# Scaling softmax exponentials on GpSimd in a two-layer encoder: a per-partition scalar operand in place of a broadcast tensor operand

## The chip, the cores and the metric

One core of one Trainium2 chip. The metric is the device time of one execution in microseconds (us), the median of several runs. Engines are named as in the profile: PE (TensorE matmul), PEld (its weight loads), DVE (VectorE), ACT (ScalarE), POOL (GpSimd), SP (SyncE, which issues nearly all DMAs).

## The reference, cut to what matters

Two layers run over 512 tokens of width 1024, in float32. Each layer projects x, mixes tokens with 16 attention heads of three kinds (6 latent heads, 6 dilated ones with a bias, 4 grouped-query ones), projects the result, normalises, and runs a SwiGLU feed-forward part. What the change touches is the softmax of each head; the grouped and latent heads compute it as

```
logits = jnp.einsum('bqkgd,bskd->bkgqs', qblk, k).astype(jnp.float32) * scale
p = jax.nn.softmax(logits, axis=-1)
return jnp.einsum('bkgqs,bskd->bqkgd', p.astype(v.dtype), v)
...
x = layer_norm(DN_ALPHA * x + mix, ln1_g[l], ln1_b[l])
ff = (jax.nn.silu(x @ ffn_w_gate[l]) * (x @ ffn_w_up[l])) @ ffn_w_down[l]
```

The dilated heads compute a mixture of three masked softmaxes, which the kernel folds into one softmax with a bias table per head.

## The kernel before, in words

A float32 product is made of three matmuls on a high and a low part of each operand (`mm3`, L159 to L167). `wload` (L142) loads a weight tile, lets ACT round it to the high part (`whi`, L152), and lets DVE or POOL subtract to get the low part (`wlo`, L156).

Attention works in units: one head and one block of 128 queries, so 64 units in a layer. `Head` has three steps for a unit. Step `a` (L236) makes the scores `sc` on PE (L241), the row minimum of the negated scores on DVE (`nm`, L247 with a bias table, L251 without one), the exponentials `pl` with their row sum on ACT (L253), the reciprocal `srec` on DVE (L255), and scales `pl` in place on POOL (L256). Step `b` (L259) transposes the scaled tile on PE (`ptr`, L264) and splits it into `PTh` (ACT, L271) and `PTl` (DVE, L272). Step `c` (L274) multiplies by the values (`po`, L282 and L283), and L288 and L290 put the halves together.

`attend` (L312) calls step `a` of unit u, step `b` of unit u-3 and step `c` of unit u-4, and between them pieces of other work, the fillers: projections of the later heads (`tp`, `qkp`, `uq`, `uv`), transposes (`tT`, `lt`), and part of the output projection (`opp`). The fillers have a due range of units in the table `W`. `evac_g1` (L460) scales and rotates a projected block `g1` on DVE (L470, L471, L474 to L477), after POOL made its `rstd` (L191, L192). `layer_norm` (L195) and `finish` close the attention part. Then comes the feed-forward part, which uses no step of `Head`.

The order of the program text isn't the order of execution. The kernel is built with `schedule_with_timeline_sim=True`: a scheduler orders the instructions of each engine by the text's priority and by what it believes each takes. On the chip each engine then works through its own list strictly in that order and waits where an operand isn't ready.

Buffers that matter here: 4 tiles for `pl` (pool `ppl`, shared with some scratch tiles), 2 PSUM banks for scores (`ps_sc`), 2 for the transposes (`ps_pt`), and one tile `gg` for the per-head gains (pool `pgg`), which is loaded again for the second layer in the middle of the first one's attention (L406) and scaled there on DVE (L407).

Of the kernel before, what the change touches and what calls it, by code (L numbers as in the profile page):

```python
# [13 lines left out]
ALU = mybir.AluOpType  # L14
AX = mybir.AxisListType

P = 128
T = 512
# [63 lines left out]
def encoder(ctx: ExitStack, tc, x, w_in, mla_q_norm, mla_kv_norm, w_uq, w_ukv, gqa_q_norm, gqa_k_norm, rel_bias,  # L82
            w_out, ln1_g, ln1_b, w_gate, w_up, w_down, ln2_g, ln2_b, tabs, onehot, neglnc, out):
    nc = tc.nc
    V, A, G, TE = nc.vector, nc.scalar, nc.gpsimd, nc.tensor
# [27 lines left out]
    def bank(pl, name):  # L113
        return pl.tile([P, 512], F32, tag="b", name=name)

    def small(n, name):
        return psm.tile([P, n], F32, tag="s", name=name)
# [44 lines left out]
    def mm3(ps, a, b, first, last):  # L162
        ah, al = a
        bh, bl = b
        TE.matmul(ps, ah, bh, start=first, stop=False)  # L165
        TE.matmul(ps, ah, bl, start=False, stop=False)  # L166
        TE.matmul(ps, al, bh, start=False, stop=last)  # L167
# [63 lines left out]
    class Head:  # L231
# [4 lines left out]
        def a(self, qt):  # L236

            sc = bank(ps_sc, "sc")
            ops = self.qk(qt)
            for i, (a, b) in enumerate(ops):  # L240
                TE.matmul(sc, a, b, start=i == 0, stop=i == len(ops) - 1)  # L241
            pl = ppl.tile([P, T], F32, tag="l", name="pl")
            nm = small(1, "nm")
            src = sc
            if self.dtile is not None:
                o = 895 - (384 - P * qt)
                V.tensor_tensor_reduce(out=pl, in0=sc, in1=self.dtile()[:, slice(o, o - T if o >= T else None, -1)], scale=1.0, scalar=3e38,  # L247
                                       op0=ALU.add, op1=ALU.min, accum_out=nm)
                src = pl
            else:  # L250
                V.tensor_reduce(nm, sc, axis=AX.X, op=ALU.min)  # L251
            s = small(1, "ssum")
            A.activation(pl, src, AF.Exp, bias=nm, scale=-1.0, accum_out=s)  # L253
            r = small(1, "srec")
            V.reciprocal(r, s)  # L255
            G.tensor_tensor(pl, pl, r.to_broadcast([P, T]), op=ALU.mult)  # L256
            self.pl[qt] = pl

        def b(self, qt):  # L259
# [133 lines left out]
    for l in range(DEPTH):  # L393
# [143 lines left out]
        def dil_qk(pair):  # L537
            ws = [wload(krows(w_in[l], 0, KD, c + pair * P, c + pair * P + P), (P, KD, P), LO['qk'], QKR[pair]) for c in (C_Q, C_K)]
            yield
            for q, (h, o) in zip((True, False), ws):  # L540
                pb = bank(ps_mm, "qkp")
                for k in range(KD):
                    mm3(pb, (h[:, k], o[:, k]), xmv(xT, k), k == 0, k == KD - 1)
                    if k % 2 and k < KD - 1:
                        yield

                if q:
                    r = pqk.tile([P, 2, T], F32R, tag="q", name="dqk")
                    sc = -(HD ** -0.5)
                    for e in range(2):  # L550
                        a, b = slice(64 * e, 64 * e + 64), slice(64 - 64 * e, 128 - 64 * e)
                        A.activation(r[a, e], pb[a], AF.Copy, scale=sc)
                        V.scalar_tensor_tensor(r[b, e], pb[a], sc, r[a, e].bitcast(F32), op0=ALU.mult, op1=ALU.subtract)
                    dqk[pair].append(r)
                else:
                    for e in range(2):
                        r = (pmix if e else pqk).tile([P, 2, T], F32R, tag="m" if e else "q", name="dk")
                        a, b = slice(64 * e, 64 * e + 64), slice(64 - 64 * e, 128 - 64 * e)
                        A.copy(r[a, 0], pb[a])
                        V.tensor_tensor(r[a, 1], pb[a], r[a, 0].bitcast(F32), op=ALU.subtract)  # L560
                        nc.sync.dma_start(r[b].bitcast(F32), r[a].bitcast(F32))
                        dqk[pair].append(r)
                yield
# [10 lines left out]
        def latent_qv():  # L574
            q = pxt.tile([P, NT, 6, 96], F32, tag="x", name="tq")
            tq.append(q)
            wq = [wload(krows(w_uq[l], 0, 2, 288 * c, 288 * c + 288), (P, 2, 288), LO['uq']) for c in range(2)]
            wkv.append(wload(krows(w_ukv[l], 0, 1, 0, 768), (P, 1, 768), LO['kv']))
            yield
            for c in range(2):  # L580
                h, o = wq[c]
                for t in range(NT):
                    pb = bank(ps_mm, "uq")[:, :288]
                    ts = slice(t * P, (t + 1) * P)
                    for k in range(2):
                        mm3(pb, (latT[k][:, 0, ts], latT[k][:, 1, ts]), (h[:, k], o[:, k]), k == 0, k == 1)
                    A.copy(q[:, t, 3 * c:3 * c + 3, :], pb.rearrange("p (h c) -> p h c", h=3))
                    yield
                tm = ppl.tile([P, T], F32, tag="l", name="qrt")[:, :384].rearrange("p (t h c) -> p t h c", t=NT, h=3)
                rope32(q[:, :, 3 * c:3 * c + 3, 64:96], 3, tm)  # L590
                told.append(("q", c))
            h, o = (w[:, 0].rearrange("p (h c) -> p h c", h=6)[:, :, HD:] for w in wkv[0])
            for t in range(NT):
                pb = bank(ps_mm, "uv")[:, :6 * HD]
                ts = slice(t * P, (t + 1) * P)
                mm3(pb, (latT[2][:, 0, ts], latT[2][:, 1, ts]), (h, o), True, True)
                vt = pv_sb.tile([P, 6, 2, HD], F32R, tag="v", name="mv")
                split_v(vt, pb.rearrange("p (a c) -> p a c", a=6))
                mv_.append(vt)
                yield  # L600

        def out_part():

            def load(half):
                wk = {}
                for k0, n in ((3, 2), (5, 1), (6, 2)):
                    w = wload(krows(w_out[l], k0, n, half * 512, half * 512 + 512), (P, n, 512), LO['opp'])
                    for j in range(n):
                        wk[k0 + j] = (w[0][:, j], w[1][:, j])
                return wk  # L610

            wk = load(0)
            yield
            for half in range(2):
                cs = slice(half * 512, half * 512 + 512)
                for t in range(NT):
                    ts = slice(t * P, (t + 1) * P)
                    pb = bank(ps_mm, "opp")
                    for i, k in enumerate((3, 4, 5, 6, 7)):
                        mm3(pb, (mix[k][:, 0, ts], mix[k][:, 1, ts]), wk[k], i == 0, i == 4)  # L620
                        if i in (1, 3):
                            yield
                    V.scalar_tensor_tensor(xt[:, t, cs], xt[:, t, cs], ALPHA, pb, op0=ALU.mult, op1=ALU.add)
                    told.append(("op", t, half))
                    if half == 0 and t == NT - 1:
                        wk = load(1)
                    yield
# [65 lines left out]
        lqv, op = latent_qv(), out_part()  # L693
# [73 lines left out]
        for part, nf in enumerate((12, 10)):  # L767
# [51 lines left out]
            for half in range(2):  # L819
# [4 lines left out]
                for toks in ((0, 1), (2, 3)) if last else ((0, 1, 2, 3),):  # L824
                    acc = [bank(ps_mm if t < 2 else ps_pv, "down") for t in toks]
                    down(acc, toks, half, LO["dl"] if last else V, LEAD if last else 0)
                    for t, pb in zip(toks, acc):
                        V.scalar_tensor_tensor(xt[:, t, cs], xt[:, t, cs], 1.0 if part else ALPHA, pb,
                                               op0=ALU.mult, op1=ALU.add)
# [35 lines left out]
```

## Time and profile before

| | us |
|---|---|
| median of 3 runs | 1281.85 (1281.53 to 1283.26) |
| the profiled execution, its own time | 1282.31 |
| span of the profiled execution | 1280.5 |
| PE busy in the span | 1250.1 |
| DVE busy | 687.7 |
| ACT busy | 543.6 |
| POOL busy | 324.6 |
| L256 on POOL, 128 instructions | 135.7 |

The span is the time from the first to the last instruction that the trace shows; the execution's own time is 1.8 us longer. Times in the trace count from the start of the span. The first layer's attention units run from about 58 to 265, the second's from about 660 to 892; the feed-forward parts lie between and behind them. Busy times of engines overlap. PE's busy time is a union of pipelined matmuls, so an interval between two matmuls says more than the duration of one.

### The profile page before, as it was taken

What the parts mean: (1) busy time and instruction counts of PE and PEld (TensorE: products, weight loads), DVE (VectorE), ACT (ScalarE), POOL (GpSimd) and SP (SyncE); (2) the same over time, 40 slices, a digit from 0 to 9 for tenths busy, and PEclk for the clock granted to TensorE, in tenths of its full rate; (3) what the DMA queues carried; (4) which work ended last, traced back from release to release, by engine and by line L of the source; (5) the groups of instructions that cost most, each with busy time, mean ns of one, the idle gap of its engine ahead of it and who ended that gap; (6) DMA issues with size and microseconds to landing.
All of it is one profiled execution on the core that took longest, in us unless ns stands there. A gap on an engine that the chain in (4) does not pass through costs nothing.

```text
span 1280.5 us, 16743 instructions
## 1 busy us (share of the span) xinstructions
PE 1250.1 (98%) x6352; PEld 1062.5 (83%) x6352; DVE 687.7 (54%) x1138; ACT 543.6 (42%) x955; POOL 324.6 (25%) x344
## 2 busy tenths in 40 slices
PE   8999899999999999999999998999999999999997
PEld 7888788889888888888898897888988888888885
DVE  4377997684333333332664889966843332333346
ACT  4465786544222212222245668855342221222222
POOL 0445475661000000000245456655500000000004
PEclk9999899999999999999999999999999999999999
DMA  5623210324333233332425231114243333333223
GB/s 179 188 67 87 87 34 13 120 69 130 99 99 97 89 96 98 99 99 99 148 78 147 84 103 48 28 30 134 77 115 99 99 99 99 99 99 98 92 96 110
DMA packets 140552, 122.57 MB, mean 96 GB/s; under 512 B 6924, under 2 KB 114572, under 8 KB 140472
## 3 DMA queue, kind: packets, MB, share of 16 engines
q1 hardware_dynamic: 140460, 121.48, 32.0%
q8 instruction: 50, 0.82, 0.3%
q14 instruction: 30, 0.25, 0.1%
q10 hardware_dynamic: 12, 0.02, 0.0%
HBM read 114.65 MB, written 2.12 MB: 91 GB/s over the span
## 4 chain that ended last, share of the span: by engine, by line
PE 80%; DVE 8%; DMA 4%; ACT 3%; POOL 2%; issue 2%; SPq 0%; DVEq 0%; POOLq 0%; ACTq 0%
PE gate L165 6%; PE down L167 6%; PE down L166 6%; PE up L167 6%; PE down L165 6%; PE up L165 6%; PE up L166 6%; PE gate L167 6%; PE gate L166 6%; PE sc L241 4%; PE ptr L264 3%; PE po L283 2%; PE po L282 2%; PE tp L166 1%; PE tp L165 1%
## 5 line engine op out<-in xcount | busy, mean ns | idle before, releaser
L152 ACT CAST whi<-wraw 128x1024 fp32r<-128x1024 f32 (+3 forms) x202 | 205.6, 1020 | 550.6 <-PE gate L166 149.3
L156 DVE TENSOR_TENSOR wlo<-wraw,whi 128x1024 fp32r<-128x1024 f32 (+3 forms) x170 | 208.2, 1226 | 319.7 <-ACT whi L152 315.7
L191 POOL TENSOR_TENSOR rstd<-mv,eps_l 128x1 f32<-128x1 f32 x16 | 5.7, 357 | 680.8 <-DVE mv L200 680.8
L256 POOL TENSOR_TENSOR pl<-pl,srec 128x512 f32<-128x512 f32 x128 | 135.7, 1061 | 153.0 <-DVE srec L255 139.2
L166 PE MATMUL gate<-xTl,whi 128*128 128x512 f32 (+1 forms) x384 | 142.8, 372 | 0.0
L166 PE MATMUL up<-xTl,whi 128*128 128x512 f32 (+1 forms) x384 | 142.7, 372 | 0.0
L167 PE MATMUL gate<-xTh,wlo 128*128 128x512 f32 (+1 forms) x384 | 142.7, 372 | 0.0
L167 PE MATMUL up<-xTh,wlo 128*128 128x512 f32 (+1 forms) x384 | 142.7, 372 | 0.0
L165 PE MATMUL up<-xTh,whi 128*128 128x512 f32 (+1 forms) x384 | 142.6, 372 | 0.0
L165 PE MATMUL gate<-xTh,whi 128*128 128x512 f32 (+1 forms) x384 | 142.4, 371 | 0.0
L167 PE MATMUL down<-whi,act 128*128 128x512 f32 x352 | 136.7, 389 | 0.0
L166 PE MATMUL down<-wlo,act 128*128 128x512 f32 x352 | 136.7, 389 | 0.0
L165 PE MATMUL down<-whi,act 128*128 128x512 f32 x352 | 136.7, 389 | 0.0
L779 DVE TENSOR_TENSOR sg<-sg,up 128x512 f32<-128x512 f32 x44 | 30.3, 688 | 136.1 <-PE up L167 134.8
L156 POOL TENSOR_TENSOR wlo<-wraw,whi 128x512 fp32r<-128x512 f32 (+2 forms) x64 | 79.4, 1265 | 78.7 <-ACT whi L152 78.4
L272 DVE TENSOR_TENSOR PTl<-ptr,PTh 128x512 fp32r<-128x512 f32 x128 | 87.2, 682 | 8.7 <-ACT PTh L271 7.6
L271 ACT CAST PTh<-ptr 128x512 fp32r<-128x512 f32 x128 | 74.9, 586 | 38.9 <-PE ptr L264 38.4
L167 PEld LDWEIGHTS up<-xTh,wlo 128*128 128x128 f32 x384 | 72.4, 189 | 12.6
L165 PEld LDWEIGHTS gate<-xTh,whi 128*128 128x128 f32 x384 | 72.3, 188 | 12.5
L166 PEld LDWEIGHTS up<-xTl,whi 128*128 128x128 f32 x384 | 72.3, 188 | 12.5
L166 PEld LDWEIGHTS gate<-xTl,whi 128*128 128x128 f32 x384 | 72.4, 188 | 12.4
L165 PEld LDWEIGHTS up<-xTh,whi 128*128 128x128 f32 x384 | 72.3, 188 | 12.4
(174 smaller groups left out, 2493.6 us busy)
## 6 DMA issues: line engine op xcount, KB each, us to landing
wraw<-in_ffn_w_down SPq DMA_DIRECT2D x54, 512.0 KB, 3.6
wraw<-in_ffn_w_up SPq DMA_DIRECT2D x44, 512.0 KB, 3.9
wraw<-in_ffn_w_gate SPq DMA_DIRECT2D x44, 512.0 KB, 3.9
wraw<-in_w_in SPq DMA_DIRECT2D x20, 512.0 KB, 4.7
wraw<-in_w_out SPq DMA_DIRECT2D x14, 512.0 KB, 3.7
dt<-tdr SPq DMA_DIRECT2D x12, 448.0 KB, 3.9
wraw<-in_w_in SPq DMA_DIRECT2D x8, 416.0 KB, 3.4
wraw<-in_w_in SPq DMA_DIRECT2D x8, 384.0 KB, 3.9
```

What stands on the lines that cost most here:

```text
L152: A.copy(h[:, :n], r[:, :n])
L156: lo.tensor_tensor(o[:, c:c + step], r[:, c:c + step], h[:, c:c + step].bitcast(F32), op=ALU.subtract)
L165: TE.matmul(ps, ah, bh, start=first, stop=False)
L166: TE.matmul(ps, ah, bl, start=False, stop=False)
L167: TE.matmul(ps, al, bh, start=False, stop=last)
L241: TE.matmul(sc, a, b, start=i == 0, stop=i == len(ops) - 1)
L256: G.tensor_tensor(pl, pl, r.to_broadcast([P, T]), op=ALU.mult)
L264: TE.transpose(pb[:, kt * P:(kt + 1) * P], pl[:, kt * P:(kt + 1) * P], ident)
L271: A.copy(ph[:, :, c:c + P], pb)
L272: V.tensor_tensor(plo[:, :, c:c + P], pb, ph[:, :, c:c + P].bitcast(F32), op=ALU.subtract)
L282: TE.matmul(po[:, h0:h0 + 256], self.vst(kt), ph[:, kt], start=kt == 0, stop=False)
L779: V.tensor_tensor(sg, sg, pss[1], op=ALU.mult)
```

## The change

The scaling of `pl` becomes a `tensor_scalar` with the column `r` as a scalar per partition; before it was a `tensor_tensor` whose second operand was `r`, repeated along the row. The result is the same product, in place.

```
             r = small(1, "srec")
             V.reciprocal(r, s)
-            G.tensor_tensor(pl, pl, r.to_broadcast([P, T]), op=ALU.mult)
+            G.tensor_scalar(pl, pl, r, None, op0=ALU.mult)
             self.pl[qt] = pl
```

No other line differs. But the scheduler orders the program anew, and the lists of all engines differ in many places. Three of them follow. The number behind a name tells one tile from another of that name.

PE in the first layer, where the grouped-query heads pass over to the latent ones (`sc_2118` is the last grouped unit's scores, `sc_2158` and `sc_2177` are the first two latent ones, `pl_2007` an earlier unit's exponentials). Before:

```order
L264 MATMUL ptr_2129<-tab_114,pl_2007 128x128 x4
L283 MATMUL po_2062<-PTl_2059,gv_801 128x256
L282 MATMUL po_2062<-PTh_2058,gv_852 128x256
L283 MATMUL po_2062<-PTl_2059,gv_852 128x256
L282 MATMUL po_2062<-PTh_2058,gv_1089 128x256
L283 MATMUL po_2062<-PTl_2059,gv_1089 128x256
L282 MATMUL po_2062<-PTh_2058,gv_1125 128x256
L283 MATMUL po_2062<-PTl_2059,gv_1125 128x256
L241 MATMUL sc_2158<-kT_2035,qkT_2001 128x512
L264 MATMUL ptr_2170<-tab_114,pl_2045 128x128 x4
```

Now:

```order
L283 MATMUL po_2062<-PTl_2059,gv_1125 128x256
L241 MATMUL sc_2177<-kT_2035,qkT_2001 128x512 x3
L264 MATMUL ptr_2129<-tab_114,pl_2007 128x128 x4
L504 MATMUL tT_2207<-tab_114,tq_1607 96x128 x4
L165 MATMUL kT_2234<-lat_1785,whi_1622 64x512
L166 MATMUL kT_2234<-lat_1785,whi_1622 64x512
L167 MATMUL kT_2234<-lat_1785,wlo_1624 64x512
L264 MATMUL ptr_2170<-tab_114,pl_2045 128x128 x4
L264 MATMUL ptr_2189<-tab_114,pl_2088 128x128 x4
L241 MATMUL sc_2215<-kT_2035,qkT_2001 128x512 x3
```

The transposes of `pl_2007` stood ahead of the scores `sc_2158`; now they stand behind `sc_2158` (which is further up) and `sc_2177`.

DVE in the first layer, around the last blocks of `g1` (`g1_1423` is the tile of blocks 2 and 3, `PTl_1456` the low part of a unit's transposed exponentials). Before:

```order
L247 ISA pl_1442,nm_1443<-sc_1439,dt_1314 128x512
L247 ISA nm_1443 128x1
L470 TENSOR_SCALAR g1_1423<-g1_1423,rstd_1429 128x256
L471 TENSOR_SCALAR g1_1423<-g1_1423,rstd_1429 128x128
L255 RECIPROCAL srec_1447<-ssum_1445 128x1
L474 TENSOR_TENSOR krt_1484<-g1_1423,tab_114 128x16
L475 TENSOR_TENSOR krt_1484<-g1_1423,tab_114 128x16
L476 TENSOR_TENSOR g1_1423<-g1_1423,tab_114 128x32
L272 TENSOR_TENSOR PTl_1456<-ptr_1500,PTh_1455 128x4x128
```

Now:

```order
L247 ISA pl_1442,nm_1443<-sc_1439,dt_1314 128x512
L247 ISA nm_1443 128x1
L272 TENSOR_TENSOR PTl_1456<-ptr_1500,PTh_1455 128x4x128
L507 TENSOR_TENSOR qkT_1544<-tT_1539,qkT_1544 128x512
L255 RECIPROCAL srec_1447<-ssum_1445 128x1
L474 TENSOR_TENSOR krt_1484<-g1_1423,tab_114 128x16
L475 TENSOR_TENSOR krt_1484<-g1_1423,tab_114 128x16
L476 TENSOR_TENSOR g1_1423<-g1_1423,tab_114 128x32
```

`PTl_1456` moved up ahead of L474 to L476; L470 and L471 moved behind, out of this piece.

POOL at the same place (`wlo_2466` is a low part of an output-projection weight). Before:

```order
L256 TENSOR_TENSOR pl_1350<-pl_1350,srec_1355 128x512
L309 TENSOR_TENSOR mix_1378<-mf_1189,mix_1378 128x512
L256 TENSOR_TENSOR pl_1396<-pl_1396,srec_1401 128x512
L191 TENSOR_TENSOR rstd_1429<-ms_1426,eps_r_118 128x2
L192 TENSOR_TENSOR rstd_1429<-rstd_1429,mhalf_117 128x2
L156 TENSOR_TENSOR wlo_2466<-wraw_2462,whi_2464 128x512 x2
L256 TENSOR_TENSOR pl_1442<-pl_1442,srec_1447 128x512
```

Now:

```order
L256 TENSOR_SCALAR pl_1350<-pl_1350,srec_1355 128x512
L156 TENSOR_TENSOR wlo_2466<-wraw_2462,whi_2464 128x512 x2
L256 TENSOR_SCALAR pl_1396<-pl_1396,srec_1401 128x512
L309 TENSOR_TENSOR mix_1378<-mf_1189,mix_1378 128x512
L191 TENSOR_TENSOR rstd_1429<-ms_1426,eps_r_118 128x2
L256 TENSOR_SCALAR pl_1442<-pl_1442,srec_1447 128x512
```

The pair of `wlo_2466` moved up by one scaling; the operation itself has changed its kind from TENSOR_TENSOR to TENSOR_SCALAR.

## Rows read from the trace of the kernel before

**Rows 1.** The page: span, and busy time of each engine with its share.
```profile
span 1280.5 us, 16743 instructions
...
PE 1250.1 (98%) x6352; PEld 1062.5 (83%) x6352; DVE 687.7 (54%) x1138; ACT 543.6 (42%) x955; POOL 324.6 (25%) x344
```

**Rows 2.** Busy us of each engine by stretch, with instructions and the granted clock.
```profile
core 0: us, PE busy (x) PEld busy (x) DVE busy (x) ACT busy (x) POOL busy (x), PEclk, DMA share, GB/s
...
300.00:600.00 300.00, 300.00 (x1356) 249.81 (x1355) 103.09 (x109) 84.42 (x102) 0.00 (x0) 1.00 0.33 99
...
58.00:265.00 207.00, 198.75 (x1159) 172.63 (x1157) 161.02 (x339) 139.46 (x312) 117.30 (x126) 0.98 0.27 77
660.00:892.00 232.00, 226.77 (x1297) 197.15 (x1297) 173.13 (x355) 155.94 (x332) 121.21 (x130) 0.99 0.29 81
...
160.00:185.00 25.00, 24.19 (x172) 22.07 (x171) 22.78 (x43) 22.76 (x54) 20.20 (x21) 1.00 0.13 43
...
230.00:265.00 35.00, 34.91 (x189) 29.06 (x187) 21.71 (x42) 21.24 (x41) 24.47 (x21) 1.00 0.50 151
```

**Rows 3.** The same view for line L256 alone: us of the stretch, POOL's busy us.
```profile
58.00:265.00 207.00, 68.25 (x64) 0.98 0.27 77
...
160.00:185.00 25.00, 11.46 (x11) 1.00 0.13 43
...
230.00:265.00 35.00, 9.37 (x8) 1.00 0.50 151
```

**Rows 4.** POOL's groups by shape (L156: 230 to 265 only): busy us, mean ns, idle.
```profile
L256 POOL TENSOR_TENSOR pl<-pl,srec 128x512 f32<-128x512 f32 x128 | 135.7, 1061 | 153.0 <-DVE srec L255 139.2 <-PE ptr L264 7.2 <-PE opp L167 6.5
...
L156 POOL TENSOR_TENSOR wlo<-wraw,whi 128x512 fp32r<-128x512 f32 x10 | 12.7, 1297 | 2.6 <-ACT whi L152 2.5
...
L192 POOL TENSOR_TENSOR rstd<-rstd,mhalf 128x2 f32<-128x2 f32 x8 | 5.6, 703 | 0.6
...
L191 POOL TENSOR_TENSOR rstd<-ms,eps_r 128x2 f32<-128x2 f32 x8 | 1.6, 195 | 0.6 <-ACT sq L468 0.6
```

**Rows 5.** What PE waited for: us in total, times, longest.
```profile
PE po L283 <- DVE PTl L272: 7.1, 6, 2.3
...
PE ptr L264 <- POOL pl L256: 2.7, 3, 2.2
```

**Rows 6.** Timeline where DVE waits for a DMA: start, us, instruction, [idle before <-releaser].
```profile
124.34 0.29 DVE L407 TENSOR_SCALAR gg<-gg 128x256 f32<-128x256 f32 x1 [5.27 <-DMA gg<-in_gqa_q_norm]
...
124.78 1.04 POOL L256 TENSOR_TENSOR pl<-pl,srec 128x512 f32<-128x512 f32 x1 [5.99 <-DVE srec L255]
...
125.87 0.66 PE L264 MATMUL ptr<-tab,pl 128*128 128x128 f32 x4 [2.21 <-POOL pl L256]
```

**Rows 7.** Timeline around PE's longest wait for PTl, and a lone L471.
```profile
127.90 0.28 DVE L471 TENSOR_SCALAR g<-g,rstd 128x128 f32<-128x128 f32 x1
...
140.97 2.55 POOL L156 TENSOR_TENSOR wlo<-wraw,whi 128x512 fp32r<-128x512 f32 x2
...
141.36 1.05 DVE L470 TENSOR_SCALAR g<-g,rstd 128x256 f32<-128x256 f32 x1
142.32 1.28 DVE L471 TENSOR_SCALAR g<-g,rstd 128x128 f32<-128x128 f32 x1
...
144.77 0.68 DVE L272 TENSOR_TENSOR PTl<-ptr,PTh 128x512 fp32r<-128x512 f32 x1
...
145.50 0.58 PE L283 MATMUL po<-PTl,dv 128*128 128x256 f32 x1 [2.31 <-DVE PTl L272]
```

**Rows 8.** Busy us by stretch again, behind that wait: the clock column.
```profile
145.00:150.00 5.00, 4.50 (x25) 4.36 (x26) 4.10 (x11) 1.78 (x4) 1.55 (x2) 0.66 0.26 97
```

More of the change, by code (lines that the diff above doesn't have):

```diff
@@ L255, in a @@
             V.reciprocal(r, s)
-            G.tensor_tensor(pl, pl, r.to_broadcast([P, T]), op=ALU.mult)
+            G.tensor_scalar(pl, pl, r, None, op0=ALU.mult)
             self.pl[qt] = pl
```

## The prediction, made before the changed kernel was run

> **What bounds the kernel now.** I read the busy times first, then the stretches, then the waits. PE is busy for 1250.1 of 1280.5 us [rows 1], so nothing that this change can do gains more than 30.4 us. The stretches show how much of that lies where scalings run. In the feed-forward part PE is busy the whole time and POOL does nothing (300 to 600 [rows 2]); the change can't touch it. In the attention stretches, 58 to 265 and 660 to 892, PE is busy for 198.75 of 207 and 226.77 of 232 [rows 2]: 8.3 and 5.2 us of idle time, and beside a clock that is granted more fully that is all there is to win. DVE, at 161.02 of 207, is the next in line, and POOL has 117.30, of which 68.25 are the 64 scalings [rows 2, 3].
>
> The mean hides the tight part. Between 160 and 185 POOL is busy for 20.20 of 25 us, DVE for 22.78 and ACT for 22.76 [rows 2], and 11.46 of POOL's time are 11 scalings [rows 3]. So POOL has 4.80 us to spare there, 0.44 for each scaling. The second layer does the same work in the same way.
>
> Is PE waiting for the scaling? Hardly: 2.7 us in all, of which one wait of 2.2 [rows 5]. And that one is not POOL's doing. The scaling at 124.78 had waited 5.99 for the reciprocal, because DVE stood for 5.27 in front of L407, whose DMA brings the second layer's gains [rows 6]. PE's larger waits, 7.1 in total, are for `PTl` [rows 5].
>
> **What the change removes and adds.** It replaces 128 TENSOR_TENSOR of 1.06 us on POOL (1.04 when undisturbed, as at 124.78) [rows 4, 6] by 128 TENSOR_SCALAR. The trace holds no TENSOR_SCALAR on POOL, so I bound its price from both sides. Below: the two-tensor subtraction of the same shape takes 1.297, and the scaling, whose second operand is one repeated column, takes 1.042 [rows 4, 6]. So not having to walk a second tensor saved 0.25; dropping the operand altogether may save as much again, which gives 0.79. Above: on POOL the kind of instruction counts more than the data. An addition on two columns takes 0.195, a power on the same two columns 0.703, a factor of 3.6 on equal bytes [rows 4]. A TENSOR_SCALAR carries two operator slots, of which the diff fills the second with None. If the engine walks the tile once for each slot, it is two passes, 2 x 1.04 = 2.08. Between 0.79 and 2.08 I take 2.08, because the pow row says that a more general kind costs a multiple and not a fraction more, and because the broadcast form is already the cheapest full-width row that POOL has. This is a choice, not a reading, and it carries the sign of the forecast; the chances below say how sure I am.
>
> The Trainium skill would choose the other end. Its page GPSIMD Engine Reference, section 4.1 (Engine selection), says that on this engine operations with two inputs are about half as fast as VectorE, while those with one input run at roughly line rate; with the 1.2 GHz of its section 1 that is an estimate of 512 / 1.2 = 0.43 us and a start-up. By it the sum would be that of the first rival, below. No row here shows a one-input operation on a full tile, so the trace can't say.
>
> **The sum for 2.08.** Each scaling is 1.04 longer.
>
> *The tight stretch.* Eleven scalings add 11.4 us to a POOL that has 4.80 to spare: 6.6 too much [rows 2, 3]. Something takes part of it up: the new order on PE. The transposes of `pl_2007` stood ahead of the first latent scores and now stand behind the first two, so POOL gets more time before PE asks. A unit takes 25 / 11 = 2.27 us of this stretch; I count one unit of room, since at this place it is two but at others less. That leaves 6.6 - 2.3 = 4.3 per layer, 8.7 for both. Behind the late transposes, `PTh`, `PTl` and `po` of that unit wait, and the scores of the next units soon lack a `pl` buffer, so PE has nothing to fill the time with.
>
> *The end of attention.* Between 230 and 265 POOL is busy for 24.47 of 35, with 8 scalings in it [rows 2, 3]: 8.3 more make 32.8 and still fit. Only the last scaling is late, with no unit behind it to cover it: 1.04 per layer, 2.1 for both.
>
> *The rest of attention.* POOL is idle for 89.7 us between 58 and 265 [rows 2]; the 64 scalings add 66.6 and fit on the whole. I cost the early units at nothing: the projections among them cover the longer latency, and if that cover were gone each late unit would cost 1.04.
>
> *The clock.* Behind PE's longest wait the granted clock reads 0.66 of full speed for 5 us [rows 8], which is part of the time at 1.2 instead of 2.4 GHz: 5 x 0.34 = 1.7 us of lost work. New waits of several us bring one such stretch per layer: 3.4.
>
> *What the order gives back.* PE's wait of 2.31 came from `PTl` at 144.77, and DVE was late with it because L470 and L471 stood ahead of it and took 1.05 and 1.28 while POOL worked on a `wlo`; alone, L471 takes 0.28 [rows 7]. In the new order `PTl_1456` stands ahead of L474 to L476, and L470 and L471 are gone from there. With a short POOL operation I would count 2.31 per layer. With a long one, DVE's instructions that wait for POOL to finish wait longer, so I count half: 1.2 per layer, -2.3 for both. The wait behind L407 I leave as it is: the same DMA ends it in either order, L407 stands at the same place in DVE's list, and what PE no longer lacks there it lacks some us later, since DVE is the one that lost the time.
>
> Together: 8.7 + 2.1 + 3.4 - 2.3 = +11.9. The profiled execution took 1282.31, 0.46 above the median of 1281.85. So 1294.2 on its scale, **1293.8 us** for the median, 0.9% slower.
>
> **The rivals.**
>
> *First rival: the new operation is short (0.79 or less) and the kernel faster.* It decides wherever the operation takes less than the 1.04 of before. POOL's list empties sooner; 16 us less per layer on POOL, nearly all off the path. What reaches the end: the waits of PE for the scaling, 2.7 at most, and the two waits of 2.31 that the new order undoes [rows 5, 7]: -7.3, giving 1274.5. For it: one operand less to fetch, and the step from 1.297 to 1.042 went the same way. The skill's line rate belongs here, and this rival's chance stands with it. Against it: the pow row.
>
> *Second rival: the price is about the same, up to 1.48, and only the order counts.* POOL then stays within its 4.80 us of spare time, the room in the new order covers the latency, and the gain is between none and the 4.6 of the two waits: -2.3 in the middle, 1279.5. For it: the operator and the tile are unchanged. DVE's load, at 161 of 207, is unchanged as well, which speaks for a small effect.
>
> *Third rival: three passes or more, over 3 us.* Then 64 x 2.08 = 133 us per layer meet 89.7 of idle time: 43 too much, 86 for both, about 1368. For it there is only the pow row; against it, that a multiplication row shows no such rate.
>
> **How the numbers follow.** The smallest effect a measurement of this kernel can tell from none is about 0.2%, 2.6 us. I give 0.42 to the forecast, 0.24 to the first rival, 0.22 to the second, 0.12 to the third. The forecast is slower in 0.34, lost in the noise in 0.06 (if the room is twice what I count, the stretch costs nothing) and faster in 0.02. The first rival is faster in 0.20 and the same in 0.04. The second is faster in 0.10, the same in 0.09, slower in 0.03. The third is slower. That is 0.32 faster, 0.19 the same, 0.49 slower. The range starts at 1273, below the first rival, and ends at 1315. That end is the forecast with an operation of 2.6: the tight stretch is then 11 x 1.56 - 4.8 - 2.3 = 10.1 over per layer, the last scaling 1.56 late, the stretch from 230 to 265 over by 24.47 + 8 x 1.56 - 35 = 2.0, and two clock stretches of 1.7 come instead of one: 30.5 for both layers, less 2.3, on 1282.31. It leaves out the third rival and the ends, under 0.2. The forecast's own range, for 1.9 to 2.6, is 1289 to 1315: at 1.9 the stretch is over by 2.4 per layer and the sum is +7.5.
>
> **What would show it.** Right: the group of L256 at about 2.1 us; POOL busy for nearly all of the stretch where the latent heads begin; PE's waits for `pl` rising from 2.7 to 10 us or more; one more low entry in the clock column per layer. Each term falls by itself: if the group reads 2.1 but the waits stay under 3, the order's room was larger than I counted; if `PTl` waits stay at 7, the order gave nothing back. Wrong in sign: a group of L256 under 1.1 us. Then PE's waits for `pl` vanish and the time is that of a rival.

## The result, and the profile after

| kernel | median us | runs | ratio to before, 95% interval |
|---|---|---|---|
| before | 1282.55 (1281.53 to 1283.35) | 4 | |
| changed | 1295.83 (1295.12 to 1297.42) | 4 | 1.0106 [1.0088, 1.0123] |

The changed kernel is 1.1% slower. The number is close to the forecast of 1293.8 and lies in its range, but most of its terms turn out wrong, as the profile already hints. The page of the changed kernel, span and busy times:

```profile
span 1293.4 us, 16705 instructions
...
PE 1254.4 (97%) x6352; PEld 1058.9 (82%) x6352; DVE 675.9 (52%) x1138; ACT 545.2 (42%) x955; POOL 390.7 (30%) x344
```

The span is 12.9 us longer, and PE's busy time grew by 4.3 only [rows 1]: the rest, 8.6, is idle time on PE. POOL has 66.1 us more. Its largest group by shape (busy us, mean ns, then the idle time ahead of it):

```profile
L256 POOL TENSOR_SCALAR pl<-pl,srec 128x512 f32<-128x512 f32 x128 | 201.7, 1578 | 99.4 <-DVE srec L255 84.6 <-PE ptr L264 5.4 <-DVE krt L475 3.9
```

128 scalings went from 1.061 us [rows 4] to 1.578, not to the 2.08 of the sum. All of POOL's growth is here: 201.7 - 135.7 = 66.0. But is PE waiting for it? The stretches that answer to [rows 2], in the changed kernel:

```profile
core 0: us, PE busy (x) PEld busy (x) DVE busy (x) ACT busy (x) POOL busy (x), PEclk, DMA share, GB/s
160.00:185.00 25.00, 22.59 (x153) 19.39 (x152) 19.86 (x40) 20.74 (x49) 23.73 (x20) 1.00 0.14 38
230.00:265.00 35.00, 34.86 (x196) 29.62 (x195) 22.77 (x45) 22.46 (x43) 26.15 (x21) 1.00 0.34 110
58.00:265.00 207.00, 195.30 (x1124) 165.68 (x1123) 150.39 (x332) 136.90 (x305) 143.29 (x122) 0.99 0.24 69
300.00:600.00 300.00, 300.00 (x1377) 250.63 (x1376) 103.31 (x111) 84.46 (x103) 0.00 (x0) 1.00 0.33 99
660.00:892.00 232.00, 222.90 (x1269) 190.98 (x1268) 162.73 (x350) 150.41 (x324) 150.19 (x127) 1.00 0.27 76
```

Between 160 and 185 POOL is now busy for 23.73 of 25 us, as foretold for an engine that becomes the bound. PE, DVE and ACT all do less there than before. That alone would fit the forecast. PE's waits in the whole trace do not (us in total, times, longest):

```profile
PE po L282 <- ACT PTh L271: 4.6, 4, 1.9
PE po L283 <- DVE PTl L272: 3.2, 7, 0.9
PE tT L504 <- DVE tq L572: 3.2, 2, 1.6
PE sc L241 <- ACT pl L253: 3.0, 6, 0.7
PE sc L241 <- DVE nm L247: 2.6, 6, 0.8
...
PE ptr L264 <- POOL pl L256: 0.3, 1, 0.3
```

PE waits for the scaled tile for 0.3 us, less than the 2.7 of before [rows 5]. What it waits for now is ACT and DVE: the scores wait for a bank whose reader hasn't run, the transposes `tT` for `tq`, the products for `PTh`. A nearly full POOL and no wait for POOL: either the price of the operation acts in a roundabout way, or it isn't the price at all.

Units 0 to 23 of a layer are the dilated heads, 24 to 39 the grouped ones, 40 to 63 the latent ones. The largest piece of new waits lies in the grouped heads and at their passage to the latent ones, called the passage below. PE's waits between 155 and 210, first in the kernel before, all there are:

```profile
PE po L283 <- DVE PTl L272: 0.8, 1, 0.8
```

and in the changed kernel:

```profile
PE tT L504 <- DVE tq L572: 1.6, 1, 1.6
PE sc L241 <- ACT pl L253: 1.5, 3, 0.7
PE po L283 <- DVE PTl L272: 0.7, 2, 0.4
PE kT L165 <- DVE qkT L507: 0.5, 1, 0.5
PE uq L165 <- DVE lat L488: 0.5, 1, 0.5
PE uv L165 <- DVE mv L366: 0.3, 1, 0.3
```

0.8 us of waits became 5.1. The second layer's passage, 785 to 850, shows the same rows, with one of 0.2 us more. So two theories stood at the start of the experiments. **Price:** the operation is 0.52 us longer and POOL, nearly full, delays the loop. **Order:** the scheduler laid out all engines' lists in a worse way, perhaps because it believes another duration of the new operation, and the time would be lost with any duration on the chip.

### The profile page after: what moved, and what is told of

It is laid out like the page before. It is cut to its first block, busy times and chain, and to the rows that moved or that the text cites. A ratio compares the mean times of both kernels' runs of the same rounds, so it can differ in the third digit from the quotient of the medians.

```text
span 1293.4 us, 16705 instructions
## 1 busy us (share of the span) xinstructions
PE 1254.4 (97%) x6352; PEld 1058.9 (82%) x6352; DVE 675.9 (52%) x1138; ACT 545.2 (42%) x955; POOL 390.7 (30%) x344
## 4 chain that ended last, share of the span: by engine, by line
PE 87%; DVE 5%; ACT 3%; DMA 2%; issue 1%; POOL 1%; SPq 0%; DVEq 0%; POOLq 0%; ACTq 0%
PE gate L166 6%; PE up L166 6%; PE gate L165 6%; PE up L165 6%; PE gate L167 6%; PE up L167 6%; PE down L165 6%; PE down L166 6%; PE down L167 6%; PE sc L241 4%; PE ptr L264 3%; PE tp L165 2%; PE tp L166 2%; PE tp L167 2%; PE po L283 2%; PE po L282 2%
## 5 line engine op out<-in xcount | busy, mean ns | idle before, releaser
L156 DVE TENSOR_TENSOR wlo<-wraw,whi 128x1024 fp32r<-128x1024 f32 (+3 forms) x170 | 203.0, 1196 | 316.8 <-ACT whi L152 312.6
L256 POOL TENSOR_SCALAR pl<-pl,srec 128x512 f32<-128x512 f32 x128 | 201.7, 1578 | 99.4 <-DVE srec L255 84.6
L156 POOL TENSOR_TENSOR wlo<-wraw,whi 128x512 fp32r<-128x512 f32 (+2 forms) x64 | 78.5, 1248 | 83.2 <-ACT whi L152 83.1
L167 PEld LDWEIGHTS gate<-xTh,wlo 128*128 128x128 f32 x384 | 72.4, 188 | 12.4
```

The lines of the kernel that those rows point to most:

```text
L156: lo.tensor_tensor(o[:, c:c + step], r[:, c:c + step], h[:, c:c + step].bitcast(F32), op=ALU.subtract)
L256: G.tensor_scalar(pl, pl, r, None, op0=ALU.mult)
```

## The experiments

Twelve kernels were run. The kernel before had a median between 1281.54 and 1282.81 in the groups of runs below; ratios are to the runs of the same group.

### Order and price taken apart

The scheduler orders by what it believes an operation takes, and the chip then works through the lists. So the operation can be exchanged behind the scheduler, with names and semaphores kept: every list stays as it is, and only the kind of 128 instructions on POOL differs. (By the tiles' names, PE's, DVE's and POOL's lists in the trace of the first such kernel are those of the changed kernel without exception.) The first kernel has the changed kernel's order and the broadcast operation of before:

```
         encoder(tc, *args)
+    for block in nc.main_func.blocks:
+        for k, i in enumerate(block.instructions):
+            if "Pool" in str(i.engine) and type(i).__name__ == "InstTensorScalarPtr" and i.ins[0].memref.startswith("pl_"):
+                r = i.ins[1].__replace__(ap=[[1, P], [0, T]])
+                block.instructions[k] = mybir.InstTensorTensor(
+                    name=i.name, engine=i.engine, debug=i.debug, ins=[i.ins[0], r], outs=list(i.outs), op=i.op0,
+                    sync_info=i.sync_info)
     return nc
```

> The program of the changed kernel, every engine in the changed kernel's order, but the 128 scalings are again the broadcast TENSOR_TENSOR. Theory price (the longer POOL operation, 1.57 instead of 1.04 us, costs the time): the group of L256 is back at 1.04 and the kernel is back near the time before, 1278 to 1284 us. Rival order (the scheduler's new order costs the time whatever the operation takes): 1292 to 1297 us, as the changed kernel. Half and half would be about 1289.

Measured: 1299.25 us (1297.84 to 1300.97, 4 runs), ratio 1.0135 [1.0121, 1.0149]. With the shorter operation back, the new order is no faster; it is 3.4 us slower than the changed kernel and above the 1297 expected.

The second is its mirror, the order of before with the per-partition operation:

```
...
+            if "Pool" in str(i.engine) and type(i).__name__ == "InstTensorTensor" and i.outs[0].memref.startswith("pl_"):
...
+                    r = i.ins[1].__replace__(ap=[[1, P], [1, 1]])
+                    block.instructions[k] = mybir.InstTensorScalarPtr(
+                        name=i.name, engine=i.engine, debug=i.debug, ins=[i.ins[0], r], outs=list(i.outs), op0=i.op,
+                        op1=ALU.bypass, sync_info=i.sync_info)
```

> The program of before, every engine in the order of before, but the 128 scalings are TENSOR_SCALAR. Theory price: at least as slow as the changed kernel, 1295 to 1305 us, since this order leaves PE less work between the scores and the transposes; PE's waits for the scaled tile rise from 2.7 us to 5 or more. Rival order: 1280 to 1285 us, as before.

Measured: 1285.89 us (1284.55 to 1287.44, 7 runs), ratio 1.0030 [1.0019, 1.0041], between the ranges of the two theories, and nearer to the order's. PE's two largest waits in it; the first is the one that the forecast had described, only smaller:

```profile
PE ptr L264 <- POOL pl L256: 7.3, 8, 2.4
PE po L283 <- DVE PTl L272: 5.8, 2, 2.9
```

So the longer operation alone costs 3.7 us, and PE's waits for `pl` rise from 2.7 to 7.3; the order alone costs 17.1. The two don't add up: together they cost 13.3, since with the longer operation the new order costs only 9.9 (1295.83 against 1285.89). The price theory explains less than a third of the loss, and in the new order it shows nothing of it.

### What the forms of the operation cost

One kernel holds four forms side by side, one for each block of queries, in an order of its own. Its last block is scaled by a constant and so isn't normalised; only the durations of its scalings are read:

```
-            G.tensor_scalar(pl, pl, r, None, op0=ALU.mult)
+            if qt == 0:
+                G.tensor_scalar(pl, pl, r, None, op0=ALU.mult)
+            elif qt == 1:
+                G.tensor_scalar(pl, pl, r, 1.0, op0=ALU.mult, op1=ALU.mult)
+            elif qt == 2:
+                for c in (0, 256):
+                    G.tensor_scalar(pl[:, c:c + 256], pl[:, c:c + 256], r, None, op0=ALU.mult)
+            else:
+                G.tensor_scalar(pl, pl, 0.5, None, op0=ALU.mult)
```

> Four forms of the scaling, one for each block of queries, on lines of their own: a TENSOR_SCALAR with one operator and the column as scalar; one with a second operator (times 1.0); two TENSOR_SCALAR on half the row each; one with the constant 0.5 in place of the column (this one leaves the normalisation out for the last block). Theory two passes (my prediction's reading of the price: a pass for each operator slot, an empty one too): the second form takes the same as the first, 1.57. Rival one pass and a dearer loop: the second form takes longer, 2 us or more. If the price is mostly a start-up, the half rows take over 1.0 each; if it is by the column, 0.85 to 0.9 each. If fetching the column as a pointer costs it, the constant form takes 1.1 or less, otherwise 1.57.

Measured, POOL's groups by shape (L257, L259, L262, L264 are the four branches in order; busy us, mean ns, idle):

```profile
L262 POOL TENSOR_SCALAR pl<-pl,srec 128x256 f32<-128x256 f32 x64 | 60.3, 952 | 37.9 <-DVE srec L255 32.4 <-PE po L291 4.5 <-PE ptr L272 0.9
L257 POOL TENSOR_SCALAR pl<-pl,srec 128x512 f32<-128x512 f32 x32 | 50.3, 1571 | 33.4 <-DVE srec L255 33.4
L264 POOL TENSOR_SCALAR pl<-pl 128x512 f32<-128x512 f32 x32 | 49.6, 1550 | 17.4 <-ACT pl L253 17.4
L259 POOL TENSOR_SCALAR pl<-pl,srec 128x512 f32<-128x512 f32 x32 | 22.8, 713 | 20.9 <-DVE srec L255 17.2 <-DVE krt L483 3.3
```

The last row decides: with a second operator, a multiplication by 1.0, the same tile takes 0.713 us, less than half of the 1.571 without it. The forecast's reading, one pass for each operator slot, is refuted, and so is the rival's, by which a second operator costs more. Why it costs less wasn't tested. The column as operand isn't what costs either: a constant takes 1.550. Halving the columns takes 0.952, so one operator costs about (1.571 - 0.952) / 256 = 2.4 ns per column.

### Three orders, three prices

If price and order are separate, a cheap form in the order of before should beat both kernels, and the same form in the changed kernel's order should not help. Both were built by the same exchange with

```
...
+                r = i.ins[1].__replace__(ap=[[1, P], [1, 1]])
+                one = mybir.ImmediateValue(dtype=F32, value=1.0)
+                block.instructions[k] = mybir.InstTensorScalarPtr(
+                    name=i.name, engine=i.engine, debug=i.debug, ins=[i.ins[0], r, one], outs=list(i.outs),
+                    op0=ALU.mult, op1=ALU.mult, sync_info=i.sync_info)
```

> Every engine keeps the order of the kernel before; only the 128 scalings on POOL become the per-partition form with two operators (times r, times 1.0), 0.694 us in the look at prices against 1.04 for the broadcast. If in this order the price acts as it did with 1.57 (3.7 us more for 0.53 us more each, mostly at units where the transposes wait for POOL), 0.35 us less each gives 1 to 3 us back: 1279.5 to 1281.5, and the waits ptr<-POOL pl and po<-PTl on PE shrink. If only the order counts, nothing changes: 1282. If the 0.694 was an effect of where it stood in that look, the L256 group shows about 1.5 and the time is 1285.9 again.

> Every engine keeps the order of the changed kernel; the scalings are the two-operator form, 0.69 us. If the order costs the time whatever the price, it stays at 1295 to 1300 though each scaling is 0.9 us shorter than in the changed kernel (and nearer to the 1299.3 of the broadcast form in that order, 1.04, if a shorter operation makes this order worse). If the price of 1.57 us is what costs the changed kernel its time, and the broadcast form loses in this order for another reason, it falls to 1283 or below.

The third order is the one that the scheduler makes when the text itself has two operators; it was run with them, and with the broadcast form put back:

```
-            G.tensor_scalar(pl, pl, r, None, op0=ALU.mult)
+            G.tensor_scalar(pl, pl, r, 1.0, op0=ALU.mult, op1=ALU.mult)
```

> The two-operator form in the text (times r, times 1.0), with the order that the scheduler then makes, a third one. If the changed kernel's loss comes from its order alone, this one may land anywhere between the first two orders, 1278 to 1300, and says how far orders lie apart. If a shorter operation decides it, 1278 to 1282.

> The third order, with the broadcast form put back (1.04 us): with the run of the two-operator form in the same order it gives the price of 0.35 us per scaling there, expected 0 to 3 us; against the kernel before it gives what the third order costs with the same operation, between -3 and +17 us if orders differ as the first two do. If the order of the changed kernel is an outlier, within 3 us of 1282.

Measured, with the two kernels above, in us and as a ratio to before:

| order made for | two operators, about 0.7 us | broadcast, about 1.06 | one operator, about 1.58 |
|---|---|---|---|
| the text before | 1276.86, 0.9951 [0.9939, 0.9964] | 1282.18 | 1285.89, 1.0030 [1.0019, 1.0041] |
| two operators | 1279.76, 0.9980 [0.9971, 0.9989] | 1286.19, 1.0027 [1.0018, 1.0036] | not run |
| the changed text | 1294.47, 1.0085 [1.0071, 1.0099] | 1299.25, 1.0135 [1.0121, 1.0149] | 1295.83, 1.0106 [1.0088, 1.0123] |

Read down a column: the changed kernel's order costs 17.1 us with the broadcast form, 17.6 with the shortest one and 9.9 with the longest. It costs most where POOL has plenty of room, so POOL's load isn't the cause. (The 1294.47 lies just under the range expected if the order decides.) The third order costs 4.0 us with the broadcast form, a little over the 3 expected, and 2.9 with two operators. Read along a row: from two operators to the broadcast form it is 5.3, 6.4 and 4.8 us, the same in every order within what these medians can tell. A shorter operation does pay, and by more than the 1 to 3 and 0 to 3 us expected. The first cell is the fastest kernel of the study, 5.3 us below before. Its scalings and what is left of PE's wait for them:

```profile
L256 POOL TENSOR_SCALAR pl<-pl,srec 128x512 f32<-128x512 f32 x128 | 90.0, 703 | 185.2 <-DVE srec L255 170.8 <-PE ptr L264 6.5 <-PE opp L167 4.9
```

```profile
PE ptr L264 <- POOL pl L256: 1.0, 1, 1.0
```

One cell doesn't fit: in the changed kernel's order the one-operator form should be slower than the broadcast form and is 3.4 us faster. The clock doesn't explain it. The trace of the broadcast form does have two low entries more than that of the changed kernel (0.66 in 180 to 185 and in 910 to 915, about 1.7 us of lost work each), but of the runs with the same mean clock, 0.997, one took 1299.77 and the other 1295.12. It stays open.

### Where the new order loses

The start of each unit's transposes, compared with the kernel before, tells where a kernel falls behind. Units are counted through both layers, 64 in each. In us, worked out from the traces, later than before:

| up to the transposes of unit | changed | new order, broadcast | order of before, one operator | order of before, two |
|---|---|---|---|---|
| 27 | 1.54 | 3.19 | 1.07 | -2.30 |
| 42 | 6.42 | 8.93 | 2.43 | -2.54 |
| 64 (second layer's first) | 5.45 | 7.69 | 3.41 | -3.28 |
| 91 | 7.18 | 11.45 | 3.81 | -5.33 |
| 106 (as 42) | 12.09 | 16.30 | 5.20 | -5.55 |
| 127 (the last) | 11.36 | 15.57 | 5.13 | -5.60 |

The changed kernel loses 4.9 us from unit 27 to 42, and 4.9 again from 91 to 106. So the passage carries about 10 of its 12.9. These marks waver by some us from unit to unit, because an order can also do other work earlier: the changed kernel is 10.09 behind at unit 45 and 3.32 at unit 63. PE's idle time in the stretch, below, doesn't hang on the choice of a unit. What is different in the passage? The scores' lead, the number of later units whose scores stand ahead of a unit's transposes on PE, counted from the lists of instructions for units 24 to 45 of the first layer:

```
before             2 2 2 2 2 3 2 3 2 3 3 3 3 3 2 2 2 2 2 2 2 3
two operators      2 2 2 2 3 3 2 3 2 3 2 3 3 3 2 2 2 2 2 2 2 2
changed            3 3 3 3 3 4 4 4 4 4 3 4 5 4 3 4 4 4 3 3 3 3
```

To test that the passage's order is enough by itself, the scheduler was shown the per-partition form for units 24 to 39 of each layer alone, and in a second kernel for units 0 to 23 alone. Then all scalings were put back to the broadcast form, so that the price is that of before (the second expectation calls units 0 to 23 grouped heads; they are the dilated ones):

```
+    CNT = [0]
...
-            G.tensor_scalar(pl, pl, r, None, op0=ALU.mult)
+            self_cnt = CNT[0]; CNT[0] += 1; u = self_cnt % 64
+            if 24<=u<40:
+                G.tensor_scalar(pl, pl, r, None, op0=ALU.mult)
+            else:
+                G.tensor_tensor(pl, pl, r.to_broadcast([P, T]), op=ALU.mult)
```

> The scheduler is shown the per-partition form for the scalings of units 24 to 39 of each layer alone (the passage from grouped to latent heads); then every scaling is put back to the broadcast form, so that only the order differs from the kernel before. The scores run three to five units ahead of the transposes from unit 28 to 43 as in the changed kernel, ahead of unit 24 all stands as before. If the loss of the new order (17 us with this form) is made in that passage, 1292 to 1299; if it is made in the units before or after it, within 4 us of 1282.

> The same for units 0 to 23 alone: the new order in the first units of the grouped heads, and in the passage a lead of two to three units, near that of the kernel before. If the passage's order costs the time, within 5 us of 1282; if the new order loses in the early units, 1290 or more.

Measured: 1297.25 us (1297.01 to 1298.78, 4 runs), ratio 1.0127 [1.0112, 1.0143], for units 24 to 39; 1287.43 us (1286.21 to 1289.43, 5 runs), ratio 1.0047 [1.0034, 1.0059], for units 0 to 23. Against the 1281.54 of before in this group that is +15.7 and +5.9; the second is just outside the 5 us expected. They add up to more than the 17.1 of the whole, so the pieces aren't independent. By the tiles' names, the lists of PE, DVE, ACT and POOL in the first kernel differ from those of before only in pieces that ran there between 155 and 204 and between 783 and 831. So the passage's order alone makes nearly all of the loss, with the operation of before. The second kernel is no such clean cut: its lists differ from 64 to 247 and from 693 to 875, in the passage too, so its 5.9 don't belong to the early units alone. The largest waits of PE in the first kernel between 155 and 210:

```profile
PE sc L243 <- ACT pl L255: 1.8, 3, 0.9
PE tT L510 <- DVE tq L578: 1.6, 1, 1.6
PE po L289 <- DVE PTl L278: 0.7, 2, 0.4
```

The same two waits lead as in the changed kernel (lines are 2 to 6 higher here). Busy times in that stretch, in this kernel:

```profile
155.00:210.00 55.00, 49.28 (x319) 41.09 (x318) 43.60 (x89) 41.66 (x98) 32.77 (x34) 1.00 0.10 25
```

in the kernel before,

```profile
155.00:210.00 55.00, 54.07 (x363) 48.01 (x362) 49.77 (x99) 46.20 (x106) 35.45 (x36) 1.00 0.08 25
```

in the changed kernel,

```profile
155.00:210.00 55.00, 49.45 (x318) 41.33 (x318) 43.63 (x89) 42.44 (x99) 45.10 (x34) 1.00 0.10 25
```

and in the kernel with the order of units 0 to 23 alone:

```profile
155.00:210.00 55.00, 53.56 (x353) 46.67 (x353) 48.57 (x101) 46.33 (x108) 36.24 (x36) 1.00 0.09 25
```

PE is idle for 5.5 to 5.7 us of the 55 in the two kernels with the new order in the passage, whether POOL is busy for 45 or for 33, and for 0.9 to 1.4 in the other two. In the changed kernel's order with the broadcast and the two-operator form it is 4.7 and 5.0, the latter with POOL busy for 25.57; in the order of before with the one-operator form it is 1.9.

How a wait arises there is seen in the timeline of the changed kernel (start, us, instruction, idle time before):

```profile
176.54 2.51 POOL L156 TENSOR_TENSOR wlo<-wraw,whi 128x512 fp32r<-128x512 f32 x2
...
177.17 0.73 PE L241 MATMUL sc<-qkT,gqT 128*128 128x512 f32 x2
...
177.84 1.62 DVE L572 TENSOR_TENSOR tq<-tq,qrt 128x384 f32<-128x384 f32 x1
179.03 1.87 POOL L256 TENSOR_SCALAR pl<-pl,srec 128x512 f32<-128x512 f32 x1
...
179.51 0.64 PE L504 MATMUL tT<-tab,tq 128*96 128x128 f32 x4 [1.61 <-DVE tq L572]
```

PE has sent its scores ahead and comes to `tT` before `tq` is ready, and nothing stands between the two in its list. DVE makes `tq` in 1.62 us, beside the second subtraction of POOL and the scaling behind it. In the kernel before, the same operation was not short either, 1.07, but DVE came to it earlier, transposes of `pl` stood between PE's scores and `tT`, and there was no wait:

```profile
174.46 1.07 DVE L572 TENSOR_TENSOR tq<-tq,qrt 128x384 f32<-128x384 f32 x1
...
175.90 0.62 PE L241 MATMUL sc<-qkT,gqT 128*128 128x512 f32 x2
176.36 0.60 PE L264 MATMUL ptr<-tab,pl 128*128 128x128 f32 x4
176.80 0.60 PE L504 MATMUL tT<-tab,tq 128*96 128x128 f32 x4
```

### Is it the scores' lead on too few buffers?

A lead of 4 or 5 wants as many `pl` tiles, and there are 4, shared with scratch. Three kernels changed that number; the scheduler then made new orders for them. For the fifth buffer, in two of them, the small statistics' pool was split to make room, which may cost something by itself:

```
-    ppl = pool("ppl", 4)
+    ppl = pool("ppl", 5)
...
-    psm = pool("psm", 12)
+    psm = pool("psm", 3)
...
-        return psm.tile([P, n], F32, tag="s", name=name)
+        return psm.tile([P, n], F32, tag="s" if n > 1 else "s1", bufs=None if n > 1 else 12, name=name)
```

> The changed kernel's text with five buffers instead of four for pl and the scratch that shares its pool (the small per-row statistics keep 12 buffers of their own, the larger ones get 3). The scheduler again puts the scores four to five units ahead of the transposes at units 28 to 42. If the loss there comes from scores so far ahead on too few buffers, the fifth gives most of it back: PE busy in 155 to 210 us from 49.5 to 52 or more, the time 1283 to 1290. If it comes from the place of other work in that order (the projections and tT), it stays at 1293 to 1299.

> The text of the kernel before with the same five buffers: the control. If a fifth buffer helps any order, it gains as much as the changed kernel does with it; if only an order with far-ahead scores wants it, 1280 to 1284.

> The changed kernel's text with three buffers: the scores can then stand only three (twice four) units ahead of the transposes at units 28 to 42, and the order is a fourth one. If it is the scores' lead that costs the changed kernel its time, the passage runs nearly as in the kernel before (PE busy in 155 to 210 us 52 or more), and the time is below 1290 unless three buffers cost elsewhere. If what counts is the number of buffers, it is slower than 1296.

Measured: changed text with five buffers 1292.27, ratio 1.0078 [1.0063, 1.0093]; text of before with five 1291.19, 1.0071 [1.0056, 1.0086]; changed text with three 1307.83, 1.0203 [1.0184, 1.0222]. None is as expected. With five buffers the changed text gains 3.6 against the changed kernel instead of about 6 or more; in its passage PE is busy for

```profile
155.00:210.00 55.00, 51.16 (x330) 43.80 (x330) 44.60 (x90) 42.95 (x98) 44.30 (x34) 1.00 0.09 25
```

that is 1.7 us more than in the changed kernel, not 2.6 or more. With three buffers the lead is down to 3 (twice 4), and it is the slowest of all, with PE at 51.19 in that stretch. The control lost 8.4 us though its lead there stays at 2 to 3. By the marks used above, from unit 27 to 42, five buffers lose 4.8 us against the kernel before, three lose 5.5 and the control 2.0. So a short lead doesn't make an order fast, and the theory of the lead and the buffers isn't confirmed. What the three do show is the spread: each order in the study that was set against the order of before with the same form of the operation was slower, by 2.9 us (1279.76 against 1276.86) to 21.9 (1307.83 against 1285.89, three buffers against four). Which pair of instructions in the passage would have to change places wasn't tried; it stays open.

## Why the prediction came out as it did

The number was right within 2.0 us and the sign was right, but by luck. The mechanism was wrong: errors of opposite sign cancelled. With the measured price of 1.58 the prediction's own steps give nothing for the tight stretch, 1.1 for the end of attention, no stretch at a low clock and -2.3 for the order, that is 1.2 us faster than before; 13.3 slower was measured.

- **"I take 2.08, because a more general kind costs a multiple."** Mis-sized: 1.578 measured, inside the bounds of 0.79 and 2.08. The reason given was wrong altogether. Two operators cost 0.713, one costs 1.571. The Trainium skill's rule on the page GPSIMD Engine Reference, section 4.1, by which one-input operations run at about line rate (estimated at 0.43 us and a start-up), is near the two-operator row only; the one-operator form of the change doesn't follow it.
- **"The tight stretch: 8.7."** POOL did become nearly full, 23.73 of 25 us. PE didn't wait for it: 0.3 us instead of 10 or more. By the prediction's own step a price of 1.58 adds 11 x 0.52 = 5.7 to a POOL with 4.80 to spare; the 0.9 too much is less than the 2.3 that it granted for the order, hence nothing. In the order of before, PE did wait for `pl` in the two passages, 1.5 us in each.
- **"I cost the early units at nothing."** In the order of before, the longer operation made PE wait eight times for `pl`, 7.3 us; 4.3 of it lie in the early units, where the kernel before has 2.7. The step failed in a small way, by 1.6, and only in that order.
- **"The end of attention: 2.1."** Not seen. From unit 42 to the last unit of the first layer the changed kernel falls no further behind: 3.32 at unit 63. It then loses 2.1 up to the second layer, but the same order with the broadcast form loses 2.3 there, so the longer operation isn't the cause.
- **"The clock: 3.4."** The sign was wrong. The changed kernel has one low entry where PE starved ahead of it, as the kernel before had [rows 8], and no other below 0.98, while the kernel before has four more. By the prediction's reckoning the low entries cost 1.7 us now and 5.1 before, so in these two executions the clock gave back about 3.4; the mean clock is 0.996 against 0.994. First the four further rows of before, then the changed kernel's:

```profile
125.00:130.00 5.00, 3.25 (x12) 2.68 (x13) 4.60 (x16) 2.57 (x8) 3.60 (x6) 0.79 0.01 2
130.00:135.00 5.00, 5.00 (x29) 4.84 (x29) 4.23 (x11) 3.87 (x9) 1.62 (x2) 0.87 0.31 83
...
770.00:775.00 5.00, 2.41 (x10) 2.21 (x11) 4.79 (x11) 3.05 (x10) 2.89 (x4) 0.80 0.35 108
775.00:780.00 5.00, 4.67 (x31) 4.10 (x30) 4.27 (x11) 3.36 (x9) 1.08 (x2) 0.86 0.32 92
```

```profile
135.00:140.00 5.00, 2.39 (x13) 1.51 (x13) 2.54 (x7) 3.73 (x8) 4.19 (x4) 1.00 0.60 186
140.00:145.00 5.00, 4.67 (x27) 4.24 (x26) 4.74 (x13) 4.67 (x16) 3.05 (x4) 0.66 0.31 107
```

- **"What the order gives back: -2.3."** This step failed outright. The two waits of 2.31 did vanish, as foretold: `PTl` waits fell from 7.1 to 3.2, the longest from 2.3 to 0.9. But the prediction looked at three places, two of them for what they would win, and took the order as a small credit. It is the term that carries the result: +17.1 us with the operation of before, +9.9 with that of the change.
- **"The wait behind L407 I leave as it is."** In the changed kernel DVE waits there for 4.94, near the 5.27 of [rows 6], but 2 us later in the trace. Roughly right.
- **The rivals.** The second said that only the order counts. It was right on the cause, though its condition, a price of up to 1.48, wasn't met, and wrong on the sign, because it priced the order by the one wait that it removes. The first named what a short operation would be worth, -7.3; the order of before with the two-operator form gained 5.3. It needed a form that the change doesn't use. The third is refuted by the price.
- **The upper end of the range.** Its sum has a slip. With two clock stretches in each layer, as its text says, the terms make 2 x (10.1 + 1.56 + 2.0 + 3.4) = 34.1, and the end is 1314; the 30.5 written there counts one and would end at 1310.5. The measured time is far from either.

## What to carry to other kernels

Where a scheduler lays out the program by its own estimates, replacing one operation can replace the order of everything, and that order can cost several times what the operation does. Take the two apart by exchanging the operation behind the scheduler, once in each order; four kernels show the price in either order and the order at either price, which need not add up, and here the best pair was one that no text produced. And price an operation in the exact form that the text will emit: the number of operators alone changed it by more than a factor of two here.

## What the runs showed of the hardware

POOL's TENSOR_SCALAR on 128x512 float32 takes 1.57 to 1.59 us with one operator and a column as scalar, 1.55 with a constant, and 0.70 to 0.73 with two operators; the broadcast TENSOR_TENSOR lies between, at 1.05 to 1.08. DVE's `tq` (L572) took 0.54 to 0.56 us wherever nothing on POOL ran beside it, and 1.59 to 1.63 in the five kernels in which POOL ran a two-tensor subtraction and then a scaling beside it; beside broadcast scalings it took anything from 0.53 to 1.37. Why wasn't tested.
